# Layer 0 attention: the last two head pairs' scores on half-array tiles, two heads side by side

## The chip, the core and the metric

The kernel runs on one core of one Trainium2 chip. Times are device microseconds of one execution. A profile is one execution taken by the hardware profiler. Its engines are PE (the matmul array; PEld is its weight load), ACT (scalar engine), DVE (vector engine), POOL (GpSimd) and SP, which issues most of the transfers. All of them take their instructions in the order in which the program was built.

## What is computed

Two layers of a hybrid backbone over 2048 latent tokens with a prefix of 256 context tokens, width 1024. Layer 0 has two branches side by side: multi-head latent attention (eight heads) and bidirectional gated linear attention (four heads, chunks). Layer 1 is a neighbourhood attention. The change touches layer 0 alone:

```python
def block_attention(q, k, v, scale):        # 8 heads, q and k of width 64 + 32, v of width 64
    s = jnp.einsum('bqhd,bkhd->bhqk', qi, k) * scale
    p = jax.nn.softmax(s, axis=-1)
    return jnp.einsum('bhqk,bkhd->bqhd', p, v)
a_x = block_attention(q_x, concat([k_x, k_c]), concat([v_x, v_c]), scale)   # latents see all 2304 tokens
a_c = block_attention(q_c, k_c, v_c, scale)                                 # context sees itself
b_x, b_c = gla_bidirectional(...)                                           # the linear branch
a = a.reshape(bsz, n, A_WIDTH) * silu(za)
```

## The kernel before

`even_attention` (line 982) goes over four pairs of heads (j = 0 to 3). A pair has five query blocks: one of 256 context queries, which sees two key tiles of 128, and four of 512 latent queries, which see all 18. One key tile for both heads of a pair is called a step here: 74 steps a pair, 296 in all.

A step's scores (lines 1097 to 1099) are three matmuls for each head. Queries and keys are split into a high and a low half in a reduced-precision float format, and a score is high x high + high x low + low x high, each over the head's 96 columns as the rows of the array (97 in the first, whose extra row adds a per-query term to the exponent). The results go to one of three PSUM banks, tile `st`. ACT takes the exponential of each head's scores (`apt`, 14 buffers). DVE adds the exponentials of each head up over the key tiles (line 1088, tiles `acc0`, `acc1`).

The value products (line 1039, `tail`) run behind: when six steps are pending, four are flushed, eight matmuls in a row. Their operand is plain f32, which leaves two records in the trace for one matmul. They have 64 output columns, so the two heads lie in the two column halves of the array and of one bank (`av`, two buffers). When a block's last step has been flushed, `finish` (line 964) sums the denominators over partitions by two matmuls into a bank of its own (`den`, one buffer), takes the reciprocal as exp(-ln) with one Newton step, multiplies by the value product and by the gate on POOL, and stores to `RT`.

The linear attention (`gla`) is woven in. Its first phase (lines 797 to 877; eighteen chunks, tile `gl`, two banks) is written ahead of the attention but placed between its steps by the scheduler of the framework, which sets each engine's order when the program is built. Each chunk passes nine short groups of matmuls and, between them, ACT, DVE and small transfers; L861 is the one group in it that uses 64 rows of the array, and L870 the last of a chunk. A scan over chunks follows (lines 903 to 908, on POOL and DVE). The second phase reads the scan's results (`enter`, line 927, and `leave`, line 945) and is called, with the split of the output weights, by `hook` at each fourth step from step 174 on.

Of the kernel before, what the change touches and what calls it, by code (L numbers as in the profile page):

```python
# [17 lines left out]
P = 128  # L18
# [14 lines left out]
A_SCALE = A_QK ** -0.5  # L33

# [54 lines left out]
class Kern:  # L89
# [673 lines left out]
    def gla(self, gp, gs, g1, gd, pp, tag):  # L763
# [159 lines left out]
        def enter(c, qT, oi, zb):  # L923

            ps = bank()
            for h in range(H):
                nc.tensor.matmul(ps[:, h * P : h * P + P], qT[:, h, :], Dl[c][:, h, :], start=True, stop=True)
# [10 lines left out]
        def leave(c, oi, zb, ss):  # L938
# [3 lines left out]
            g.tensor_tensor(out=oi[:], in0=oi[:], in1=zb, op=ALU.mult)  # L942
            ps = bank()
            for h in range(H):
                nc.tensor.transpose(ps[:, h * P : h * P + P], oi[:, h * P : h * P + P], self.ident[:])
# [5 lines left out]
        def second():  # L951

            order = self.back_order()
            old, cur = None, fetch(order[0])
            for c in order[1:] + [None, None]:
                if old:
                    leave(*old)
                old = enter(*cur) if cur else None
                cur = fetch(c) if c is not None else None
                yield  # L960
# [21 lines left out]

    def even_attention(self, ap, pp, hook):
# [13 lines left out]
        def keys(j, p):  # L997

            K[j, p] = kh = ring[(3 * j + p) % 4]
            for a, b in parts(j, p):  # L1000
                nc.sync.dma_start(kh[:A_QK, :, a:b].bitcast(F32),
                                  self.KT[2 * j : 2 * j + 2, 0, :A_QK, p * W + a : p * W + b].rearrange("h p t -> p h t"))
                yield

        def low(j, p):
            L[j, p] = kl = self.tl(ap, [P, 2, W], "akl", F32R, bufs=3)
            for a, b in parts(j, p):
                nc.sync.dma_start(kl[:A_QK, :, a:b].bitcast(F32),
# [14 lines left out]
        def queries(j, q0, w):  # L1023

            q = self.tl(ap, [P, 4, w], "aq" if w == 512 else "aqc", F32R, bufs=2 if w == 512 else 1)
            nc.sync.dma_start(q[:A_QK, :, :].bitcast(F32), self.QT[2 * j : 2 * j + 2, :, :A_QK, q0 : q0 + w].rearrange("h z p t -> p (h z) t"))
# [4 lines left out]
        pend, late, O = [], [], {}  # L1031

        def tail(j, nb, n, kt, pts):

            w, kts = blocks[nb][1:]
            if n == 0:
                O[j, nb] = self.tl(pp, [P, 512], "av", bufs=2)
            for i in range(2):
                nc.tensor.matmul(O[j, nb][i * 64 : i * 64 + 64, :w], V[j, kt // TT][:, kt % TT, i * 64 : i * 64 + 64], pts[i][:, :w],  # L1039
                                 start=n == 0, stop=n == len(kts) - 1)  # L1040
            if n == len(kts) - 1:
                late.append([1, j, nb])

        def end(j, nb):
# [3 lines left out]
            self.finish(O.pop((j, nb))[:, :w], sums.pop((j, nb)), zt[:, :w], self.RT[j, :, q0 : q0 + w], w, ap, pp, ("den", 1))  # L1048

        def step_late():  # L1050
            for x in late:
                x[0] -= 1
                if x[0] <= 0:
                    end(*x[1:])
            late[:] = [x for x in late if x[0] > 0]

        early, sums, first = {}, {}, {}
        for j in range(4):
# [12 lines left out]
            for nb, (q0, w, kts) in enumerate(blocks):  # L1071
# [8 lines left out]
                acc = [self.tl(ap, [P, 512], f"acc{i}") if nb else self.tl(ap, [P, CTX], f"accc{i}", bufs=1) for i in range(2)]  # L1080

                def add(n, pts):
                    for i in range(2):
                        if n == 0:
                            first[i] = pts[i]
                        else:
                            a = first[i] if n == 1 else acc[i]
                            self.add = nc.vector.tensor_tensor(out=acc[i][:, :w], in0=a[:, :w], in1=pts[i][:, :w], op=ALU.add)  # L1088

                for n, kt in enumerate(kts):  # L1090
                    pts = []
                    kq = slice(kt % TT * P, kt % TT * P + P)
                    kh, kl = K[j, kt // TT], L[j, kt // TT]
                    for i in range(2):
                        qh, ql = Q[:, 2 * i, :], Q[:, 2 * i + 1, :]
                        ps = self.tl(pp, [P, 512], "st", bufs=3)
                        nc.tensor.matmul(ps[:, :w], kh[: A_QK + 1, i, kq], qh[: A_QK + 1, :w], start=True, stop=False)  # L1097
                        nc.tensor.matmul(ps[:, :w], kh[:A_QK, i, kq], ql[:A_QK, :w], start=False, stop=False)  # L1098
                        mm = nc.tensor.matmul(ps[:, :w], kl[:A_QK, i, kq], qh[:A_QK, :w], start=False, stop=True)  # L1099
                        pt = self.tl(ap, [P, 512], "apt", bufs=14)  # L1100
                        ex = self.act(pt[:, :w], ps[:, :w], AF.Exp, scale=A_SCALE)
                        pts.append(pt)
                    add(n, pts)
                    if n == len(kts) - 1:
                        sums[j, nb] = [a[:, :w] for a in acc]
                    pend.append((j, nb, n, kt, pts))
                    with self.tc.issue_after(mm.ins):
                        if len(pend) == 6:
                            step_late()
# [883 lines left out]
```

## Time and profile before

| | |
|---|---|
| time, median of three runs | 3546.57 us (3543.09 to 3547.34) |
| span of the profiled execution | 3541.8 us |
| PE busy in it | 3477.8 us, 98% |
| DVE, ACT, POOL busy | 2392.1, 1398.4, 1214.3 us |
| attention stage, first to last score matmul | 1058.5 to 1887.1 us |
| score matmuls in the trace (lines 1097 to 1099) | 576 of 512 columns on each line, 16 of 256 |
| records of value products | 1184 |

A group of the profile reads: line, engine, operation, tile written and tiles read, rows * columns of the array, shape of the operand, count, then busy time, mean length of one in ns, and idle time of the engine ahead of it with what ended it. In a row in order of time the first two numbers are the start and the length from the first start to the last end of what the row merges, in us.

### The profile page before, as it was taken

Reading aid. Unit: us, or ns where it says so; the run is one execution under the profiler, and the core shown is the slowest. Engines: PE = TensorE matmul, PEld = TensorE weight load, DVE = VectorE, ACT = ScalarE, POOL = GpSimd, SP = SyncE. Lnnn points to the kernel's source line nnn. Section 1 sums busy time; section 2 is a strip of 40 time slices with the busy share of each in tenths; the row PEclk is TensorE's granted clock in tenths of the full one; section 3 lists DMA queues with packets and bytes.
Section 4 is the critical chain, followed back from the end, with each engine's and each line's share of the span. In section 5 each row is a group of like instructions: output and inputs, shape, how many; then the busy total and the mean of one; then the engine's idle time right before and its main releaser. Section 6 shows DMA issues by size and latency. Waiting matters only on the chain. (4 is left out here: it accounts for less than half of the span.)

```text
span 3541.8 us, 53493 instructions
## 1 busy us (share of the span) xinstructions
PE 3477.8 (98%) x19260; PEld 2752.4 (78%) x19260; DVE 2392.1 (68%) x5020; ACT 1398.4 (39%) x2656; POOL 1214.3 (34%) x1363
## 2 busy tenths in 40 slices
PE   8999999999999999999999999999999999999999
PEld 6998999999996666656667888888898987555587
DVE  4677767888886777788765345455598883777821
ACT  5555451111116555555553134444422223555510
POOL 1433330111111222211321233333354544777743
PEclk9999999999999999999999999999999999999999
DMA  6555564222243343434543554555844348878664
GB/s 246 161 148 169 149 196 116 78 76 85 68 124 83 80 111 85 101 84 115 161 119 126 169 174 124 143 161 156 255 152 146 123 128 224 217 210 218 187 184 149
DMA packets 386914, 513.75 MB, mean 145 GB/s; under 512 B 61229, under 2 KB 264061, under 8 KB 380746
## 3 DMA queue, kind: packets, MB, share of 16 engines
q1 hardware_dynamic: 353242, 418.68, 41.3%
q0 software_dynamic: 21888, 62.56, 5.9%
q10 hardware_dynamic: 11520, 29.09, 2.3%
q8 instruction: 153, 2.51, 0.3%
q14 instruction: 111, 0.91, 0.1%
HBM read 330.61 MB, written 179.59 MB: 144 GB/s over the span
## 5 line engine op out<-in xcount | busy, mean ns | idle before, releaser
L1088 DVE TENSOR_TENSOR acc<-acc,apt 128x512 f32<-128x512 f32 x512 | 379.6, 772 | 142.2 <-ACT apt L106 139.5
L739 DVE TENSOR_REDUCE mm<-mx 128x1 f32<-128x512 f32 (+1 forms) x656 | 390.8, 628 | 87.8 <-PE mx L738 80.4
L106 ACT ACTIVATE apt<-st 128x512 f32<-128x512 f32 (+1 forms) x592 | 344.8, 594 | 247.3 <-PE st L1099 207.5
L1039 PE MATMUL av<-apt,av 128*64 128x512 f32 (+1 forms) x1184 | 270.0, 592 | 0.0
L1097 PE MATMUL st<-aq,akh 97*128 97x512 f32 x576 | 245.1, 426 | 1.0 <-ACT apt L106 1.0
L738 PE MATMUL mx<-mk,mq 96*128 96x512 f32 (+1 forms) x656 | 241.7, 371 | 0.0
L106 ACT ACTIVATE u<-gm 128x352 f32<-128x352 f32 (+1 forms) x144 | 70.8, 493 | 418.4 <-PE gm L131 182.6
L1098 PE MATMUL st<-aq,akh 96*128 96x512 f32 x576 | 228.2, 396 | 0.0
L1099 PE MATMUL st<-aq,akl 96*128 96x512 f32 x576 | 227.9, 396 | 0.0
L106 ACT ACTIVATE opt<-opt 128x930 f32<-128x930 f32 (+9 forms) x144 | 119.5, 831 | 254.5 <-POOL opt L1856 140.0
L1039 PEld LDWEIGHTS av<-apt,av 128*64 128x64 f32 x1184 | 80.1, 136 | 152.7 <-issue 149.7
L1554 DVE CUSTOM_DVE_ANT_1 mx<-mx,mtab 128x465 f32<-128x465 f32 (+12 forms) x576 | 180.3, 341 | 26.5 <-PE mx L1548 20.4
L1689 POOL TENSOR_TENSOR oacc<-oacc,opt 128x682 f32<-128x682 f32 (+9 forms) x144 | 170.3, 1200 | 40.6 <-ACT opt L106 39.1
L1818 DVE TENSOR_TENSOR opt<-st,tab 128x64 f32<-128x64 f32 (+10 forms) x576 | 142.3, 312 | 37.8 <-PE st L1654 33.2
L1097 PEld LDWEIGHTS st<-aq,akh 97*128 97x128 f32 x576 | 108.3, 188 | 72.6 <-issue 44.6
L1099 PEld LDWEIGHTS st<-aq,akl 96*128 96x128 f32 x576 | 109.5, 190 | 25.2
L738 PEld LDWEIGHTS mx<-mk,mq 96*128 96x128 f32 x656 | 123.3, 188 | 6.0
L1098 PEld LDWEIGHTS st<-aq,akh 96*128 96x128 f32 x576 | 109.9, 191 | 17.0
L106 ACT ACTIVATE x<-px,modB,modA 128x128 f32<-128x128 f32 x272 | 98.7, 465 | 55.9 <-PE px L362 32.5
L129 PE MATMUL gm<-w1h,hhi 128*128 128x512 f32 x288 | 115.1, 400 | 0.0
L1653 PE MATMUL st<-q,kt 128*128 128x480 f32 (+5 forms) x256 | 98.4, 386 | 16.8 <-DVE opt L1818 13.1
L131 PE MATMUL gm<-w0h,hlo 128*128 128x512 f32 x288 | 113.3, 393 | 1.5 <-DVE hlo L392 1.5
(602 smaller groups left out, 10275.6 us busy)
## 6 DMA issues: line engine op xcount, KB each, us to landing
q<-Q SPq DMA_DIRECT2D x48, 512.0 KB
H<-x ACTq DMA_DIRECT2D x36, 512.0 KB
adaw<-ada_w SPq DMA_DIRECT2D x64, 256.0 KB
x<-H SPq DMA_DIRECT2D x32, 512.0 KB
K1t<-okt POOLq DMA_DIRECT2D x32, 512.0 KB, 6.8
kt<-K1t SPq DMA_DIRECT2D x32, 512.0 KB
mtab<-rpb_q SPq DMA_DIRECT2D x16, 899.0 KB
QT<-qkhl SPq DMA_DIRECT2D x36, 384.0 KB
```

Of the source, the lines that this page charges most:

```text
L106: return self.nc.scalar.activation(out, in_, func, **kw)
L129: self.nc.tensor.matmul(out, lh(k), rh(k), start=j == 0, stop=False)
L738: mm = nc.tensor.matmul(ps[:, :w], q[:A_QK, (t % 6) * P : (t % 6) * P + P], k[:A_QK, k0 : k0 + w], start=True, stop=True)
L739: nc.vector.tensor_reduce(out=m[:, t, n : n + 1], in_=ps[:, :w], axis=AX.X, op=ALU.max)
L1039: nc.tensor.matmul(O[j, nb][i * 64 : i * 64 + 64, :w], V[j, kt // TT][:, kt % TT, i * 64 : i * 64 + 64], pts[i][:, :w], start=n == 0, stop ...
L1088: self.add = nc.vector.tensor_tensor(out=acc[i][:, :w], in0=a[:, :w], in1=pts[i][:, :w], op=ALU.add)
L1097: nc.tensor.matmul(ps[:, :w], kh[: A_QK + 1, i, kq], qh[: A_QK + 1, :w], start=True, stop=False)
L1098: nc.tensor.matmul(ps[:, :w], kh[:A_QK, i, kq], ql[:A_QK, :w], start=False, stop=False)
L1099: mm = nc.tensor.matmul(ps[:, :w], kl[:A_QK, i, kq], qh[:A_QK, :w], start=False, stop=True)
L1554: nc.vector.tensor_tensor_reduce(out=s, in0=s, in1=tb[:, ri : ri + rn, ci : ci + cn], scale=1.0, scalar=-3e38, op0=ALU.add, op1=ALU.max, a ...
L1689: self.psum = nc.gpsimd.tensor_tensor(out=a, in0=a, in1=pts[:, :, a0 - r0 : a1 - r0, :], op=ALU.add)
L1818: badd = nc.vector.tensor_tensor(out=pt[:, d[0], d[1]], in0=ps[:, d[0], d[1]], in1=tabs[j][i][:, ri : ri + rn, ci : ci + cn], op=ALU.add)
```

## The change

- For head pairs 2 and 3 (`HALVES`) a head's operands lie in 64 partitions, head 0 in the lower and head 1 in the upper half. A score is then five matmuls: three products of the 64 columns without rotary part (keys' low tile `kl` now holds high and low of these), one of 64 rows that holds two products of the 32 rotary columns, and one of 33 rows with the third and the extra row. The heads' matmuls alternate, each head into its own bank.
- The loads of these pairs are cut to match: six plus two transfers for a part of the keys instead of one plus one, twelve for a block of queries instead of two. POOL writes one row of ones into four key tiles.
- Score tiles get four banks. The bank comes from the denominators: ACT copies a block's value product out (`take`), the denominators are then summed into the same bank (`divide`), and `newton` does the rest.
- Exponentials of both heads share a tile, and so do the sums: one add of 1024 columns for a step.
- A flush is a chain in fixed order, scores wait in the program's order for the last flush and for the second phase's matmuls, and `hook` calls the second phase at a flush (`enter`, then `leave` of the chunk before) and at its middle (`scale`).

```diff
@@ even_attention: loads of pairs 2 and 3
+                if j >= HALVES:
+                    c = slice(p * W + a, p * W + b)
+                    for i in range(2):
+                        r, src = i * 64, self.KT[2 * j + i, :, A_NOPE:A_QK, c]
+                        for u, z in ((0, 0), (0, 1), (1, 0)):
+                            nc.sync.dma_start(kh[r + z * A_ROPE : r + z * A_ROPE + A_ROPE, u, a:b].bitcast(F32), src[z])
...
+                    for i in range(2):
+                        nc.sync.dma_start(kl[i * 64 : i * 64 + 64, :, a:b].bitcast(F32),
+                                          self.KT[2 * j + i, :, :A_NOPE, p * W + a : p * W + b].rearrange("z p t -> p z t"))
@@ scores
+                for k, kz, qz, n in ((kl, 0, 0, 64), (kl, 0, 1, 64), (kl, 1, 0, 64), (kh, 0, 2, 64), (kh, 1, 3, A_ROPE + 1)):
+                    for i in range(2):
+                        r = slice(i * 64, i * 64 + n)
+                        with self.tc.issue_after(mm.ins) if mm else ExitStack():
+                            mm = nc.tensor.matmul(ps[i], k[r, kz, kq], Q[r, qz, :w], start=qz == kz == 0 and k is kl, stop=k is kh and kz == 1)
@@ denominators
+    def take(self, o, pool, bufs):
+        y = self.tl(pool, [P, 512], "oy", bufs=bufs)[:, : o.shape[1]]
+        self.taken = self.act(y, o)
+        return y
+    def divide(self, o, acc, pool, bufs):
+        for h, a in enumerate(acc):
+            self.den = self.nc.tensor.matmul(o[h * 64 : h * 64 + 64], self.mtwos[:], a, start=True, stop=True)
...
+        def flush():
+            mm = None
+            jobs = [(ending, *x) for x in taken]
+            taken.clear()
+            for _ in range(4):
+                if pend and pend[0][2] == 0 and len(busy) == 2:
+                    break
+                if pend:
+                    jobs.append((tail, *pend.pop(0)))
...
+            for f, *a in jobs:
+                with self.tc.issue_after(mm.ins) if mm else ExitStack():
+                    mm = f(*a)
+            return mm
@@ the step
-                        ps = self.tl(pp, [P, 512], "st", bufs=3)
...
+                    ps = [self.tl(pp, [P, 512], "st", bufs=4)[:, :w] for _ in range(2)]
+                    mm = score(j, kt, Q, ps, w)
+                    pt = self.tl(ap, [P, 2, 512], "apt", bufs=7)
...
+                        self.add = nc.vector.tensor_tensor(out=acc[:, :, :w], in0=(first if n == 1 else acc)[:, :, :w], in1=pt[:, :, :w], op=ALU.add)
@@ hook
-                    if count[0] >= 174 and count[0] % 4 == 2:
+                    if count[0] >= 174 and (full or mid and said[0] == "A"):
                         with self.tc.issue_after(mm.ins), self.tc.issue_after(ex.ins), self.tc.issue_after(self.add.ins):
-                            next(slow, None)
+                            for _ in range(1 + (full and said[0] == "A")):
+                                said[0] = next(slow, None)
```

The order on PE shows what moves. First pair 3, before, between two flushes (`st` scores, `gl` the linear attention's second phase: `goi` is `leave`, `D` is `enter`):

```order
L1098 MATMUL st_16956<-aq_16634,akh_1774_10751 128x512
L1099 MATMUL st_16956<-aq_16634,akl_16423 128x512
L945 MATMUL gl_16905<-ident_58,goi_16703 128x128 x4
L927 MATMUL gl_16916<-D_1801_10808,gqT_16833 128x128 x4
L1097 MATMUL st_16962<-aq_16634,akh_1774_10751 128x512
```

and the same phase of the program now, at a flush (`av` value products):

```order
L1165 MATMUL st_16728<-aq_16582,akh_1773_10750 128x512
L1000 MATMUL av_16668<-accc_16511,mtwos_63 64x256 x2
L1098 MATMUL av_16750<-apt_16606,av_15555 64x512 x2
L1098 MATMUL av_16750<-apt_16623,av_15555 64x512 x2
L1098 MATMUL av_16750<-apt_16641,av_15555 64x512 x2
L1098 MATMUL av_16750<-apt_16657,av_15555 64x512 x2
L928 MATMUL gl_16767<-D_1802_10809,gqT_16698 128x128 x4
L949 MATMUL gl_16781<-ident_58,goi_16578 128x128 x4
L1165 MATMUL st_16798<-aq_16582,akl_16345 128x512
L1165 MATMUL st_16799<-aq_16582,akl_16345 128x512
```

The second phase has moved from between scores to between a flush and scores, and the scores of a step alternate between two banks (here 16798 and 16799).

In the first half of pair 2 the first phase of the linear attention cuts into flushes; this is one flush, now:

```order
L1098 MATMUL av_14949<-apt_15079,av_14761 64x512
L819 MATMUL gl_12093<-gG_12044,trr_10789 128x4x64
L820 MATMUL gl_12093<-ge_12046,trr_10789 128x4x64
L819 MATMUL gl_12093<-gG_12044,trr_10789 128x4x64
L820 MATMUL gl_12093<-ge_12046,trr_10789 128x4x64
L1098 MATMUL av_14949<-apt_15079,av_14761 64x512
L1098 MATMUL av_14949<-apt_15095,av_14761 64x512
L862 MATMUL gl_12108<-gqT_12066,gkT_12067 128x128
L1098 MATMUL av_14949<-apt_15095,av_14761 64x512
L1098 MATMUL av_14949<-apt_15119,av_14761 64x512 x2
L1098 MATMUL av_14949<-apt_15135,av_14761 64x512 x2
```

Its eight value products stand in pieces of one, two and five. Before, three flushes in the whole stage were cut after an odd number.

More of the change, by code (lines that the diff above doesn't have):

```diff
@@ L33 @@
 A_SCALE = A_QK ** -0.5
+HALVES = 2
 AXES = ((32, 8, 8), (64, 16, 16))
@@ L1047, in end @@
             nc.sync.dma_start(zt[:, :w], self.zaT[j, :, q0 : q0 + w])
[L1048 to L1057, printed above, removed]
+            rest.append((j, nb, o, y, rc, zt[:, :w]))
+            return self.den
@@ new lines, in behind @@
+        def behind(*last):
+            with ExitStack() as es:
+                for x in last:
+                    es.enter_context(self.tc.issue_after(x.ins))
+                for j, nb, o, y, rc, zt in rest:
+                    self.newton(o, y, rc)
+                    nc.gpsimd.tensor_tensor(out=rc, in0=rc, in1=zt, op=ALU.mult)
+                    q0, w, _ = blocks[nb]
+                    nc.sync.dma_start(self.RT[j, :, q0 : q0 + w], rc)
+                    busy.remove((j, nb))
+                rest.clear()
+                if late and not taken:
+                    taken.append((*late[0], self.take(late.pop(0)[2], ap, 1)))
```

146 lines of the change are left out of this document (93 added, 53 removed).

## The prediction

> **What bounds the kernel now.** The change lies in one stage, the layer 0 attention, so I read that stage first: busy time by head pair (columns: stretch, length, busy time and record count of PE, PEld, DVE, ACT, POOL, granted clock, DMA share, GB/s).
>
> ```profile
> 1058.50:1268.50 210.00, 207.77 (x1043) 130.90 (x1042) 155.48 (x219) 125.72 (x242) 42.44 (x49) 1.00 0.37 95
> 1268.50:1498.50 230.00, 227.46 (x1197) 144.59 (x1196) 169.37 (x236) 132.68 (x260) 62.78 (x65) 1.00 0.36 88
> 1498.50:1697.00 198.50, 197.43 (x931) 119.48 (x929) 167.10 (x286) 109.91 (x202) 35.94 (x33) 1.00 0.42 113
> 1697.00:1887.10 190.10, 190.10 (x902) 118.08 (x901) 131.16 (x280) 110.04 (x218) 42.91 (x42) 1.00 0.40 114
> ```
>
> PE is busy for 99% of the four pairs, at full clock (1.00). DVE, the next, has 69 to 84%, ACT 55 to 60%. The row of matmuls on PE sets the end of the stage, so the change is priced in PE time, and the other engines count where they make PE wait. The groups:
>
> ```profile
> L1039 PE MATMUL av<-apt,av 128*64 128x512 f32 (+1 forms) x1172 | 267.4, 592 | 0.0
> L1097 PE MATMUL st<-aq,akh 97*128 97x512 f32 x576 | 245.1, 426 | 1.0 <-ACT apt L106 1.0
> L861 PE MATMUL gl<-gqT,gkT 64*128 64x128 f32 x288 | 27.7, 289 | 0.0
> L870 PE MATMUL gl<-gu,gat 128*128 128x128 f32 x144 | 19.6, 279 | 1.9 <-DVE gat L866 1.8
> ```
>
> The mean there is a record's latency. What a matmul costs is the distance to the next start, in order of time:
>
> ```profile
> 1517.15 0.40 PE L1099 MATMUL st<-aq,akl 96*128 96x512 f32 x1
> 1517.48 1.16 PE L861 MATMUL gl<-gqT,gkT 64*128 64x128 f32 x14
> 1518.57 0.50 PE L1097 MATMUL st<-aq,akh 97*128 97x512 f32 x1
> 1518.90 0.40 PE L1098 MATMUL st<-aq,akh 96*128 96x512 f32 x1
> 1519.14 0.40 PE L1099 MATMUL st<-aq,akl 96*128 96x512 f32 x1
> 1519.37 0.40 PE L1097 MATMUL st<-aq,akh 97*128 97x512 f32 x1
> ...
> 1730.76 0.60 PE L945 MATMUL gl<-ident,goi 128*128 128x128 f32 x4
> 1731.20 1.06 PE L927 MATMUL gl<-D,gqT 128*128 128x128 f32 x8
> 1732.01 0.48 PE L1097 MATMUL st<-aq,akh 97*128 97x512 f32 x1
> ...
> 1735.37 0.40 PE L1099 MATMUL st<-aq,akl 96*128 96x512 f32 x1
> 1735.69 3.65 PE L1039 MATMUL av<-apt,av 128*64 128x512 f32 x16
> 1739.28 0.50 PE L1097 MATMUL st<-aq,akh 97*128 97x512 f32 x1
> 1739.62 0.39 PE L1098 MATMUL st<-aq,akh 96*128 96x512 f32 x1
> ```
>
> Three things are to be seen. A 512-column score matmul costs 0.235 us (0.24 and 0.23 between starts). The value product's 16 records, two for each of eight matmuls, take 3.59 us to the next start, 0.43 for two records: the heads, in column halves of the array, run side by side. And each change of tile form costs: 0.32 instead of 0.235 from score to value product, 0.34 for the first score after it.
>
> **The change part by part.**
>
> *Scores.* In pairs 2 and 3 a step (one key tile, two heads) goes from six matmuls one after another to five pairs on row halves. Whether such pairs overlap the trace shows at L861, the one form on 64 rows: 14 records, alternating between the halves, take 1.16 us, while eight records of L927 on the whole array take 1.06, or (1.06 - 0.28) / 7 = 0.11 each. Fourteen in a row would be 0.28 + 13 x 0.11 = 1.71; eight slots with a slow first of 0.1 are 1.15. So they overlap, in f32 at 128 columns; for these operands at 512 columns no row shows it. The bounds are a pair at 0.235 and at 0.47; I take 0.235, the end to which the nearest row belongs. There are 144 steps of 512 columns and four of 256, half as dear: 144 x 0.235 + 4 x 0.12 = 34.3 us saved.
>
> *Tile changes.* Scores in pairs 2 and 3 now have another form than the full-array matmuls of linear attention between them. Those were free: 1730.76 to 1732.01 is 1.25 us for 12 records of 0.11. Counted in the program's order from the first score to the last value product, changes of form go from 222 to 288: into value products and denominators 83 to 93, into scores 94 to 109, into other full-array work 13 to 60, into L861's 32 to 26. Prices from the rows: into a value product 0.14 (0.085 ahead of it and 0.05 on its first record), into scores 0.20 (0.10 of the 3.59, and 0.34 instead of 0.235 on the first), into L861 0.19, into full-array work 0.15, between those. 10 x 0.14 + 15 x 0.20 + 47 x 0.15 - 6 x 0.19 = +10.3 us.
>
> *Split flushes.* More flushes are now cut by other work after an odd number of matmuls, and the one without a partner has the array alone:
>
> ```profile
> 1403.90 3.60 PE L1039 MATMUL av<-apt,av 128*64 128x512 f32 x14
> 1407.43 0.66 PE L847 MATMUL gl<-ident,gqt 128*128 128x128 f32 x4
> 1408.02 1.07 PE L1039 MATMUL av<-apt,av 128*64 128x512 f32 x2
> 1409.02 0.66 PE L847 MATMUL gl<-ident,gkt 128*128 128x128 f32 x4
> ```
>
> Seven matmuls take 3.53 and the eighth 1.00, 4.53 against 3.59 for eight together; less the extra change of form that is 0.43 for each odd piece. Before there are 6 such pieces, now 25, and two of half the width: 19 x 0.43 + 0.4 = 8.6, and 0.7 for six odd pieces of paired scores: +9.3 us.
>
> *Four banks.* Heads now use banks two by two, so a step waits for both exponentials of the step two back. ACT's and PE's rows in order of time:
>
> ```profile
> 1614.05 1.55 ACT L106 ACTIVATE apt<-st 128x512 f32<-128x512 f32 x3
> ...
> 1614.30 0.40 PE L1099 MATMUL st<-aq,akl 96*128 96x512 f32 x1
> 1614.68 0.50 PE L1097 MATMUL st<-aq,akh 97*128 97x512 f32 x1
> 1615.01 0.40 PE L1098 MATMUL st<-aq,akh 96*128 96x512 f32 x1
> ...
> 1732.57 0.40 PE L1099 MATMUL st<-aq,akl 96*128 96x512 f32 x1
> ...
> 1733.00 3.40 ACT L106 ACTIVATE apt<-st 128x512 f32<-128x512 f32 x5 [0.41 <-PE st L1099]
> ```
>
> Three exponentials take 1.55, so they follow each other by 0.475 and one lasts 0.60; the first starts 0.03 after its matmul's end (1732.97 to 1733.00). A pair of banks started at t has its last matmuls at t + 0.94, done at 1.34, exponentials from 1.37 and 1.85, the second done at 2.45. A score that had waited for one began 0.05 after its end (1614.05 + 0.60 to 1614.68, with rounding) and its next came 0.33 later, 0.10 slow. The bank is free at 2.50; PE comes for it at 2 x 1.175 = 2.35. The third step of a run is held by 0.15 and up to 0.10 more, and all of PE's row behind it; the fourth is not. 28 flush cycles lie behind the linear attention's first phase: 28 x 0.20 = +5.6 us, bounds 0 and 37 x 0.25 = 9. ACT's throughput suffices: 0.95 us of exponentials in a step of 1.175.
>
> *Denominators.* They move from a bank of their own into the block's, after a copy on ACT. Inside the stage the copy is a flush old when PE comes; the 20 copies of 0.6 us fit into ACT's 40% of idle time. At the very end nothing covers it:
>
> ```profile
> 1889.50 3.65 PE L1039 MATMUL av<-apt,av 128*64 128x512 f32 x16
> 1892.99 1.03 PE L970 MATMUL den<-acc,mtwos 128*64 128x512 f32 x4
> ```
>
> From the last value record's start: 0.59 latency, 0.03, 0.60 copy, 0.05 = 1.28 instead of 0.43: +0.9 us.
>
> *Linear attention.* Its first phase ends later in the program: six of its 18 chunks now pass L870's matmuls in pair 2, three before.
>
> ```profile
> L870 PE MATMUL gl<-gu,gat x144: 272/275/377, 1136.5 to 1547.9; 128*128 128x128 f32 x144
> ```
>
> That is 24.2 us a chunk over 17 intervals. In the new pair 2 they lie 7.1 steps apart: 7.1 x (1.175 + 0.86) + 5 of its own matmuls + some 3.5 of changes and odd pieces = 23. PE comes up to 1.2 us early for each, if the chain over ACT, DVE and DMA can't go faster: bounds 0 and 8 us, I take +2, since the 1.9 us of L870 over all chunks show a chain that mostly keeps up.
>
> *Sums, loads.* One 1024-wide add takes the place of two:
>
> ```profile
> L1088 DVE TENSOR_TENSOR acc<-acc,apt x512: 674/691/2455, 1066.0 to 1888.1; 128x512 f32<-128x512 f32 x171
> ...
> L1258 DVE TENSOR_TENSOR aq<-pr,aq x2: 1224/1224/1225, 1844.6 to 1889.1; 128x1024 fp32r<-128x1024 f32 x2
> ...
> L1026 SPq DMA_DIRECT2D aq<-QT x3: 320/444/456, 1693.9 to 1798.4; - x3
> ```
>
> 1.22 against 2 x 0.69, on an engine with idle time: nothing on the path. SP issues 116 more transfers, at 0.44 some 50 us of its queue, spread over the last two pairs; queries are loaded a block (about 45 us) ahead, so 12 issues instead of 2 cost nothing. If that lead were gone, 10 x 0.44 = 4.4 us a block would show. POOL gets four one-row memsets, and is idle for 70% and more.
>
> *Sum.* -34.3 + 10.3 + 9.3 + 5.6 + 0.9 + 2 = -6.2 us. The profiled execution spans 3541.8 us, so 3535.6; the median of the runs lies 4.8 above that span: **3540.4 us**.
>
> **The rivals.** A measurement here tells a change from none at about 0.2%, 7.1 us, so below 3539.5 is faster and above 3553.7 slower.
>
> (1) *More of the saving stays* (18%). The third step isn't held, because exponentials end earlier than their records, and the chain keeps up: -34.3 + 10.3 + 9.3 + 0.9 = -13.8, 3533; if strict order also removes half of some 8 us in which PE stands now (the stage's 828.6 us against 821 of slots, changes and odd pieces added up as above), 3529. For it: ACT's slack. Against: the bank's arithmetic is only 0.15 short but short each time.
>
> (2) *Row halves don't overlap fully* (10%). [...] One by one, ten matmuls cost 2.35 against 1.41: 144 x 0.94 + 2 = +137 in place of -34.3, with no hold by banks: 3546.6 + 137 + 10 + 9 + 1 = 3704. The point from which the scores lose is a pair at 6 x 0.235 / 5 = 0.28. Of the 10%, four are for a partial loss, a pair at 0.31: 144 x (1.55 - 1.41) + 0.4 = +20.6, no hold, 3589 with the other terms. For it: no row for this form. Against: L861, whose slots are no longer than those of the whole array. [...]
>
> (3) *The wait moves to linear attention* (17%). In pair 2 PE stands ahead of chunk matmuls, since scores between them now pass in less time. From 13 us of such waits beside the forecast's it is slower: two us at each of six chunks and a few at the ends. Six at 3 us more: 3558. For it: 23 against 24.2. Against: chunks' pace before was set by PE's own order.
>
> **How the numbers follow.** Forecast 55%, own range 3532 to 3550, split about evenly by the bound, which lies 0.9 us below it. Faster: 0.25 of that, and 0.17 from (1): 0.42. Slower: 0.10, 0.11 and 0.03 from (2), (3) and the forecast: 0.24. The rest, 0.34, is the same. The range reaches from (1)'s far end with a margin for the unknown banks, 3523, to (3) with 8 us more, 3566; it leaves out (2) and some tails.
>
> **What would show it.** Right: pairs of score records some 0.01 us apart and pairs 0.235 apart; the four pairs at about 200, 221, 217 and 185 us, since chunks move from the first two to the third; a hold of 0.15 to 0.25 at each third step; odd pieces at 1.0 us for two records. Wrong: pairs at 0.3 or more; idle time of PE named after DVE or ACT at L871 and the transposes; a wait for a query's load.

## The result and the profile after

The changed kernel takes 3590.81 us (median of four runs, 3588.79 to 3594.35); the kernel before, run on the same chip, 3544.83. The ratio, here and below always to the kernel before on the same chip, is 1.0135, 95% interval 1.012 to 1.0149: **slower by 46 us**, where 6 us less were forecast, and outside the range of 3523 to 3566. The profiled execution spans 3587.0 us.

The busy time by head pair (stretch, length, then busy time and records of PE, PEld, DVE, ACT and POOL, granted clock, DMA share, GB/s), changed kernel:

```profile
1060.00:1258.80 198.80, 197.78 (x959) 123.33 (x958) 127.00 (x134) 118.03 (x225) 40.74 (x40) 1.00 0.35 89
1258.80:1479.00 220.20, 217.57 (x1099) 136.34 (x1097) 142.79 (x151) 124.81 (x243) 59.01 (x54) 1.00 0.34 85
1479.00:1733.10 254.10, 227.61 (x1402) 132.53 (x1401) 186.87 (x246) 122.65 (x247) 68.80 (x56) 0.94 0.39 104
1733.10:1932.20 199.10, 187.90 (x1204) 108.89 (x1203) 138.51 (x215) 105.21 (x226) 50.78 (x43) 0.97 0.42 120
```

About 200, 221, 217 and 185 us were forecast. The first two pairs came out as forecast; the third is 37 us longer, the fourth 14. In these two PE stands: it is busy for 90% and 94% instead of 99% and 100%, and the granted clock is below 1.00. What it stands for, in the list of PE's waits from 1300 us to the stage's end (who <- for whom, us in total, times, longest):

```profile
PE st L1165 <- ACT apt L107: 15.7, 4, 6.2
PE av L1000 <- ACT oy L107: 8.3, 3, 6.0
PE gl L949 <- POOL goi L943: 7.6, 1, 7.6
PE gl L804 <- DVE ge L865: 6.3, 2, 4.6
```

ACT is idle for half of these stretches, so "ACT" is not the cause. Its rows in order of time, each of which starts just before a long wait of PE ends (in brackets: idle time before, and what ended it):

```profile
1641.93 0.63 ACT L107 ACTIVATE gG<-wraw 128x512 fp32r<-128x512 f32 x1 [9.12 <-DMA wraw<-w_out]
...
1757.22 0.38 ACT L107 ACTIVATE oy<-av 128x256 f32<-128x256 f32 x1 [3.89 <-DVE rc L1012]
...
1884.91 0.63 ACT L107 ACTIVATE woh<-wraw 128x512 fp32r<-128x512 f32 x1 [9.05 <-DMA wraw<-w_out]
```

ACT kept to the order of its queue: PE had ended four scores by 1636.9, and their exponentials, behind the split at 1641.93, started at 1642.46. Twice it stands in the split of an output weight whose load could start only when DVE had finished the split before (there is one buffer `wraw`), once in the copy `take`, for whose single buffer `oy` DVE's Newton step is late. The first of the two is late because of DVE, which began its part of the previous split 5.6 us after ACT had done its own. At the second, near the stage's end, DVE was in time: SP issued the load 2 us later, behind three other loads, and ACT could start 7.3 us after that. The exponentials behind the splits, and the denominators behind the copy, are what PE then waits for. The longest wait, 7.6 us, is for the second phase's `scale`, which comes through DVE and POOL while DVE is still in the backward scan. Two more are long. One of 4.6 us, at 1500.5, is a chunk's own chain: DVE, which makes the `ge` that L804 waits for, had stood 3.9 us for the transfer `gE<-gqt`. One of 3.6 us, at 1685.7, stands behind ACT's copy in `leave`, whose tile `gsb` has its two buffers in common with the backward scan.

Why these meet now, two rows of single lines show (durations, then first and last start):

```profile
L871 PE MATMUL gl<-gu,gat x144: 272/275/377, 1138.6 to 1631.4; 128*128 128x128 f32 x144
...
L909 DVE TENSOR_TENSOR D<-gsb,fac x17: 687/689/1637, 1159.5 to 1687.6; 64x512 f32<-64x512 f32 x17
```

The first phase of linear attention ends at 1631 us; before it was 1548. Its last chunk stands at step 192 in the program's order, before at step 163.5, while splits and second phase still begin at step 174. So the last chunks, the scan (to 1688), the splits and the second phase's first chunks (from 1660) lie on top of each other. Who has no room for that is DVE. The scan's stretch by busy time, in the kernel before and then in the changed one:

```profile
1548.00:1614.00 66.00, 66.00 (x284) 38.56 (x283) 63.73 (x95) 35.76 (x60) 1.65 (x1) 1.00 0.22 58
```

```profile
1631.00:1690.00 59.00, 41.66 (x237) 24.75 (x238) 55.02 (x81) 19.18 (x38) 7.81 (x6) 0.84 0.25 71
```

DVE (third busy time) was full here before, 97%, and PE just did not wait. Now it is at 93%, with other work in the stretch and faster steps of PE beside it, and PE is busy for 71%.

Each long wait costs a second time. The one of 6.2 us, PE in order of time and then the granted clock by stretch:

```profile
1635.57 0.85 PE L1165 MATMUL st<-aq,akl 64*128 64x512 f32 x6
1636.25 0.62 PE L1165 MATMUL st<-aq,akh 64*128 64x512 f32 x4
1643.10 2.13 PE L1165 MATMUL st<-aq,akl 64*128 64x512 f32 x6 [6.22 <-ACT apt L107]
1644.60 1.48 PE L1165 MATMUL st<-aq,akh 64*128 64x512 f32 x4
```

```profile
1636.90:1640.50 3.60, 0.00 (x0) 0.00 (x0) 3.44 (x6) 0.00 (x0) 0.00 (x0) 0.99 0.10 12
1640.50:1647.30 6.80, 4.21 (x19) 3.22 (x20) 5.98 (x9) 3.82 (x8) 0.00 (x0) 0.50 0.33 109
1647.30:1654.00 6.70, 6.70 (x43) 3.20 (x40) 6.58 (x8) 3.20 (x7) 1.78 (x1) 1.00 0.13 39
```

Before the wait three pairs of scores take 0.68 us, behind it 1.50: the clock is granted at one half for 6.8 us, from 3.6 us after PE fell idle. There are six such stretches in the stage, 44 us in all, and none in the kernel before.

**The balance of pairs 2 and 3.** They are 51 us longer than forecast (453 against 402). Gaps of PE of more than 0.8 us beyond a record's normal distance make 39 us (before: none in these pairs). The 107 records at half clock took 28 to 30 us where the same forms at full clock take 17, 11 to 13 more, by how a record's normal distance is taken. That leaves 1 us or less: the other terms of the sum were right together, which does not say that each of them was.

### The profile page after: what moved, and what is told of

The parts are those of the page before. It is cut to its first block, busy times and chain, and to the rows that moved or that the text cites. A ratio compares the mean times of both kernels' runs of the same rounds, so it can differ in the third digit from the quotient of the medians.

```text
span 3587.0 us, 54227 instructions
## 1 busy us (share of the span) xinstructions
PE 3484.8 (97%) x19852; PEld 2738.3 (76%) x19852; DVE 2362.2 (66%) x4744; ACT 1392.5 (39%) x2676; POOL 1252.4 (35%) x1367
## 4 chain that ended last, share of the span: by engine, by line
PE 82%; DVE 6%; DMA 6%; issue 2%; ACT 2%; POOL 1%; SPq 0%; POOLq 0%; DVEq 0%; ACTq 0%
PE gm L132 8%; PE gm L130 8%; PE gm L131 8%; PE av L1098 7%; PE st L1165 4%; PE mx L739 4%; PE gm L191 2%; PE gm L192 2%; PE gm L193 2%; PE st L1751 2%; PE st L1156 2%; PE st L1158 2%; PE o L1781 2%; PE st L1157 2%; PE st L130 2%
## 5 line engine op out<-in xcount | busy, mean ns | idle before, releaser
L1201 DVE TENSOR_TENSOR acc<-acc,apt 128x1024 f32<-128x1024 f32 x256 | 354.3, 1384 | 164.6 <-ACT apt L107 157.6
L107 ACT ACTIVATE apt<-st 128x512 f32<-128x512 f32 (+1 forms) x592 | 327.5, 597 | 176.2 <-PE st L1158 91.0
L1098 PE MATMUL av<-apt,av 128*64 128x512 f32 (+1 forms) x1184 | 285.2, 602 | 0.0
L1165 PE MATMUL st<-aq,akl 64*128 64x512 f32 x864 | 153.3, 424 | 15.7 <-ACT apt L107 15.7
L1165 PEld LDWEIGHTS st<-aq,akl 64*128 64x128 f32 x864 | 88.8, 193 | 59.5 <-ACT apt L107 27.1
L1156 PE MATMUL st<-aq,akh 97*128 97x512 f32 x288 | 121.6, 422 | 1.0 <-ACT apt L107 1.0
L1157 PE MATMUL st<-aq,akh 96*128 96x512 f32 x288 | 114.6, 398 | 0.0
L1158 PE MATMUL st<-aq,akl 96*128 96x512 f32 x288 | 114.6, 398 | 0.0
L223 POOL TENSOR_TENSOR oss<-oss,mhalf 128x8 f32<-128x8 f32 x68 | 112.5, 1654 | 5.5
L130 PE MATMUL gm<-w0h,hhi 128*128 128x512 f32 x288 | 114.3, 397 | 0.0
```

Of the source, the lines that this page charges most:

```text
L107: return self.nc.scalar.activation(out, in_, func, **kw)
L130: self.nc.tensor.matmul(out, lh(k), rh(k), start=j == 0, stop=False)
L1098: mm = nc.tensor.matmul(O[j, nb][i * 64 : i * 64 + 64, :w], V[j, kt // TT][:, kt % TT, i * 64 : i * 64 + 64], pt[:, i, :w], start=n == 0, ...
L1156: nc.tensor.matmul(ps[i], kh[: A_QK + 1, i, kq], qh[: A_QK + 1, :w], start=True, stop=False)
L1157: nc.tensor.matmul(ps[i], kh[:A_QK, i, kq], ql[:A_QK, :w], start=False, stop=False)
L1158: mm = nc.tensor.matmul(ps[i], kl[:A_QK, i, kq], qh[:A_QK, :w], start=False, stop=True)
```

## The experiments

All kernels compute the whole function. Theory A: linear attention's late first phase, and the waits that come of it, eat the saving. Theory B: the 64-row tiles, or what they need, make the waits.

**Without 64-row tiles; then with their number of loads.**

```diff
-HALVES = 2
+HALVES = 4
```

> The restructured program with full-array scores in all four pairs (no 64-row tiles, and the loads of before). Theory A, the loss comes from linear attention: its first phase now ends 28 steps later in the program, so its last chunks, the scan, the weight splits and the second phase, which starts at a fixed step, meet in pairs 2 and 3, and PE waits for them. Here the first phase ends at step 200, later still, so the waits stay and the 34 us of the scores are given back: 3595 to 3625 us, with at least four PE waits above 3 us. Theory B, the 64-row tiles and what they need (twelve transfers for a block of queries, banks two by two) make the waits: 3535 to 3560, no wait above 3 us.

The second run adds to this, for keys and likewise for their low halves and the queries:

```diff
+                if j >= 2:
+                    for i in range(2):
+                        for m in range(3):
+                            s = slice(32 * m, 32 * m + 32)
+                            nc.sync.dma_start(kh[s, i, a:b].bitcast(F32), self.KT[2 * j + i, 0, s, p * W + a : p * W + b])
```

> As the run without 64-row tiles, but the loads of pairs 2 and 3 are cut into as many transfers as the 64-row tiles need (six and two for a part of the keys, twelve for a block of queries, by groups of rows and the same bytes). Theory A: the same time as the run without them, within 8 us. Theory B: SP's queue holds back what linear attention loads and stores; at least 15 us longer than that run.

3587.6 us without the tiles (ratio 1.0128, 1.0113 to 1.0143), 3587.4 with their loads. So the loss is there without a single 64-row tile, and SP's extra transfers cost nothing: Theory B falls. Theory A's time was too high too, by 7 us at its lower end, and three waits of 3 us or more are there where it named at least four; they stand at other places than in the changed kernel. PE's waits of the first run:

```profile
PE gl L928 <- ACT gsb L107: 17.4, 1, 17.4
PE av L1000 <- ACT oy L107: 7.1, 3, 5.3
PE gl L949 <- POOL goi L943: 3.0, 1, 3.0
```

With the first phase at step 200 the second phase runs into the scan even harder: one wait of 17.4 us, in which ACT's copy gets a `gsb` buffer only when the scan gives it back.

```profile
1701.78 2.18 ACT L107 ACTIVATE gsb<-gl,gn 128x128 f32<-128x128 f32 x8 [18.22 <-DVE gsb L908]
```

**What made the first phase late.** Which part of the change moved it was read from the order of programs built with one part undone at a time; these were not run, and no trace shows their steps. Scores tied to the last flush or not, a flush in fixed order or not: the last chunk stays at 192. Two adds instead of the joined one: 186. Three score banks instead of four: 159. In the traces of pairs 0 and 1 a chunk takes mostly 10 to 12 steps in the changed kernel, 8 in the kernel before. The likely reason, which no run shows by itself, is that the fourth bank lets the scheduler place scores further ahead, so that the chunks' short groups fall back. In pairs 0 and 1 nothing needs the fourth bank. So:

```diff
-                    ps = [self.tl(pp, [P, 512], "st", bufs=4)[:, :w] for _ in range(2)]
+                    ps = []
+                    for _ in range(2):
+                        tag = ("st", "st", "st2")[nst[0] % 3] if j < BANKS else ("st", "st2", "st", "st3")[nst[0] % 4]
+                        ps.append(self.tl(pp, [P, 512], tag, bufs=2 if tag == "st" else 1)[:, :w])
+                        nst[0] += 1
```

> The changed kernel with one edit: pairs 0 and 1 use three of the four score banks in rotation, pairs 2 and 3 all four. Built so, the scheduler places the first phase of linear attention as before: its last chunk ends at step 162 (before 163.5, changed kernel 192), changes of tile form in the stage fall from 290 to 245 and odd pieces of value products from 26 to 6. Theory A: the waits above 3 us go, the saving of the scores stays, 3515 to 3535 us, pairs of about 208, 228, 185 and 180 us. Theory B: pairs 2 and 3 keep their waits, 3575 to 3595.

3558.5 us (1.0048, 1.0032 to 1.0065): by the ratios 31 of the 46 us come back with this edit alone, and the trace has the last chunk at step 162. Not all of this is waits. From the first to the last score the profiled stage is 28 us shorter than in the changed kernel. PE's gaps above 0.8 us account for 17 of them (21 instead of 38), and about 10 are PE's own row, with the gaps and half of the busy time at half clock taken off. That row has 244 changes of tile form instead of 289 (222 in the kernel before) and 6 odd pieces of value products instead of 25 (6 before); at the prediction's prices the difference is 45 x 0.15 + 19 x 0.43 = 15 us. So the late first phase cost in two ways, and Theory A names one of them. The same edit in the program without 64-row tiles (`BANKS = HALVES = 4`):

> The restructured program with full-array scores in all pairs and three of the four score banks in rotation in all of them; the first phase ends at step 163 as before. Against the run without 64-row tiles it undoes the fourth bank alone. Theory A (the fourth bank made the first phase late): the waits above 3 us around the scan go, 3545 to 3562 us, and against the run with 64-row tiles and three banks in pairs 0 and 1 it shows what these tiles bring: 0 to 20 us. Rival (the 64-row tiles are what is left of the loss): 3535 to 3545, faster than that run by 13 us or more.

3568.1 us (1.0073, 1.0059 to 1.0087), 19.5 less than without the edit. So the fourth bank in pairs 0 and 1 is shown as the largest cause with the tiles; without them it makes 19.5 of 45 us, and the rest is not told apart. The first time lies between the two theories' ranges, the second above both: more waits than thought were left. Between these two runs the tiles bring about 9 us by the ratios. Pairs 2 and 3 of the run with tiles:

```profile
1501.40:1703.00 201.60, 193.68 (x1235) 112.55 (x1234) 165.03 (x215) 102.09 (x206) 41.76 (x37) 0.97 0.40 109
1703.00:1903.20 200.20, 188.79 (x1206) 109.76 (x1203) 138.53 (x215) 105.34 (x226) 50.85 (x43) 0.97 0.41 119
```

Still 8 and 11 us of idle PE, and 0.97 of the clock.

**The collisions undone, with the first phase left late** (splits from step 186 on and the last one a block later, the copy two steps later, the factors' exponential a chunk later, one scan operation on POOL):

```diff
-                    if count[0] >= 174 and (full or mid and said[0] == "A"):
+                    if count[0] >= 186 and (full or mid and said[0] != "B"):
...
-                if late and not taken:
+                if late and not taken and wait[0] < 0:
...
-                    eng.tensor_tensor(out=d[sl], in0=S[sl], in1=f[sl, 1, :]
+                    nc.gpsimd.tensor_tensor(out=d[sl], in0=S[sl], in1=f[sl, 1, :]
```

> The changed kernel, its first phase as late, with the collisions undone one by one: the weight splits start 12 steps later, two to a flush; the last of them comes one block later; the exponential of the decay factors is taken one chunk after their load; the copy of a value product waits two steps after a Newton step; POOL takes one of the three operations of the backward scan. Theory A: the waits at these five places (4.7, 6.4, 11.4, 6.1, 5.3 us in the changed kernel) fall below 2 us each, 3545 to 3562 us. Theory B: at most 10 us of the time comes back, 3578 to 3592.

3581.4 us (1.0113, 1.0098 to 1.0128), a miss for Theory A: 9 us came back. That is Theory B's range, though B's own reason had fallen with the runs before. The waits did not go, they changed their names:

```profile
PE st L1176 <- ACT apt L107: 10.0, 3, 6.4
PE gl L956 <- DVE goi L936: 7.2, 1, 7.2
PE gl L956 <- POOL goi L950: 6.1, 1, 6.1
PE av L1105 <- DVE rc L1019: 5.8, 2, 5.1
```

Behind most of this stands DVE, late with its adds, splits and the scan; and POOL's share of the scan made DVE wait up to 1.2 us for POOL in a chunk. Removing a wait at the one who waits was of little use while DVE was late.

**The waits left in the run with three banks, one by one.** The copy's buffer:

```diff
-                    taken.append((*late[0], self.take(late.pop(0)[2], ap, 1)))
+                    taken.append((*late[0], self.take(late.pop(0)[2], ap, 2)))
...
-            zt = self.tl(ap, [P, 512], "azt", bufs=2)
+            zt = self.tl(ap, [P, 512], "azt", bufs=1)
```

> As the run with three banks in pairs 0 and 1, and the copy of the value product has two buffers instead of one (the gate's tile one instead of two). Theory A: the wait of 6.1 us at the third change of pair, where ACT stands for the one buffer until DVE's Newton step has read it, falls below 2 us; 3548 to 3555 us. Rival: the Newton step's own end, which frees the value product's bank, is what is late; the wait moves to the next value product, 3556 to 3561.

3555.2 us (1.0039, 1.0025 to 1.0052), between the two forecasts. ACT's wait is gone, and the rival's mechanism was right: the wait is now PE's own, for the bank that the same Newton step frees.

```profile
PE av L1099 <- DVE rc L1013: 4.7, 1, 4.7
```

The splits' pace:

```diff
-                    for _ in range(6):
+                    for _ in range(3):
                         next(ws)
                         yield "W"
+                        yield "W"
                     for n, k in enumerate(second):
-                        if n % 4 == 3 and n < 36:
+                        if n % 3 == 2 and n < 36:
...
+                        with self.tc.issue_after(self.add.ins):
+                            for _ in last_w[0]:
+                                pass
```

> As the run with three banks in pairs 0 and 1, and the weight splits are paced by half at first (every second flush, then one in every three calls of the second phase) and the last one comes behind the last block. Theory A: the waits of 2.7 and 5.5 us, where ACT stands in a weight split for a load that could only start when DVE had done the split before, go; 3546 to 3553 us. Rival: ACT is late at these places for other reasons, 3556 to 3561.

3553.7 us (1.0035, 1.0021 to 1.0048), between the two forecasts. The wait of 2.7 us went; the last split's stayed, 5.2 us after 5.4. The likely reason is that it was tied to an add, which orders DVE's queue and not ACT's; tied to the last exponential, below, it went. Both remedies together, the Newton step ahead of the next add, and one scan operation on POOL:

```diff
+                      with self.tc.issue_after(self.newt.ins) if self.newt else ExitStack():
                         self.add = nc.vector.tensor_tensor(out=acc[:, :, :w], in0=(first if n == 1 else acc)[:, :, :w], in1=pt[:, :, :w], op=ALU.add)
```

> The changed kernel with three banks in pairs 0 and 1, two buffers for the copy, paced weight splits, the Newton step ahead of the next add on DVE, and one of the three operations of the backward scan on POOL. Theory A: no wait of PE above 3 us is left between the first score and the last, the clock stays granted in full, and the saving of the prediction appears: 3523 to 3540 us. Rival: something else than these waits holds the time, and 3545 or more is left.

3548.4 us (1.0019, 1.001 to 1.0028): better, but the rival's side. POOL's share made DVE wait for POOL about 1 us in each chunk of the scan. Mended:

```diff
+        with self.tc.issue_after(self.gat.ins):
+            scan(self.back_order(), slice(64, 128), nc.vector, "gsb")
...
+                        with self.tc.issue_after(self.ex.ins):
+                            for _ in last_w[0]:
+                                pass
```

> The run with all remedies, mended where its trace showed new waits: the backward scan is DVE's again but starts behind the last chunk's masks, and the last weight split is queued on ACT behind the last exponential. Theory A (waits of PE, and nothing else, ate the saving): the waits of 2.5 and 3.7 us at the scan and at the last split go, one of about 2.4 at the third change of pair stays; 3528 to 3541 us. Rival: something else holds the time, 3545 or more.

3543.6 us (1.0004, 0.9995 to 1.0013): level with the kernel before, between the two forecasts. The same with `HALVES = BANKS = 4`:

> The same remedies with full-array scores in all pairs and three of four banks throughout: the one difference to the run before is the 64-row tiles of pairs 2 and 3. By the prediction's prices, with 35 more changes of tile form, six odd pieces and the hold of the banks, the tiles bring 34 - 6 - 3 - 6 = 19 us: theory A 3545 to 3560 us, 12 to 22 above that run. Rival (the tiles bring nothing, since DVE and ACT can't follow the faster steps): within 6 us of it.

3550.0 us (1.0028, 1.0017 to 1.004): the tiles bring 6.4 us here by the medians and 8.5 by the ratios, whose intervals leave some 3 to 14. So they bring something, and the numbers don't decide between the rival's 6 and Theory A's 12. Added up over records in pairs 2 and 3, score matmuls take 20 us less with tiles than without, all other matmuls 5 more, and the waits above 0.8 us 5 more: PE, faster through its steps, waits more. So the rival's reason holds for a part, and the scores' price too.

**Two adds instead of the joined one**, in the run with three banks:

```diff
+                        for i in range(2):
+                            self.add = nc.vector.tensor_tensor(out=acc[:, i, :w], in0=(first if n == 1 else acc)[:, i, :w], in1=pt[:, i, :w], op=ALU.add)
```

> As the run with three banks in pairs 0 and 1, but two adds of 512 columns instead of one of 1024. The place of the first phase stays (its end at step 162). If the joined adds, which DVE cannot interrupt for a split or a mask, make the waits that are left: 3544 to 3552 us. If not: 3555 to 3563.

3566.2 us (1.0073, 1.0059 to 1.0086), slower: the joined add is not the trouble.

**The scan.** In the level kernel ACT's rows name what is late:

```profile
1599.62 1.09 ACT L108 ACTIVATE apt<-st 128x512 f32<-128x512 f32 x2 [5.96 <-DVE acc L1208]
...
1604.26 1.08 ACT L108 ACTIVATE apt<-st 128x512 f32<-128x512 f32 x2 [3.03 <-DVE acc L1208]
```

The exponential has no free buffer, since DVE is behind with its adds by as many steps as there are buffers, seven. So one chunk of the scan was dealt out behind every second add:

```diff
+                    if count[0] >= 163 and count[0] % 2:
+                        with self.tc.issue_after(self.add.ins):
+                            next(self.backward, None)
```

> As the run with mended remedies, but the backward scan is dealt out, one chunk behind every second step's add from step 163 to 197, instead of as fast as DVE gets to it. Theory A (the two waits of 2.3 and 2.6 us, where an exponential's buffer isn't free since DVE is behind with its adds, come from scan work packed between adds): both fall below 1.5 us and the clock stays granted there; 3533 to 3540 us. Rival: DVE has no room for the scan at this pace wherever it stands; the waits move within the scan's stretch, 3541 to 3548.

and with it, in a run of its own:

```diff
-                    eng.tensor_tensor(out=d[sl], in0=S[sl], in1=f[sl, 1, :]
+                    nc.gpsimd.tensor_tensor(out=d[sl], in0=S[sl], in1=f[sl, 1, :]
```

> As the run with the scan dealt out, and POOL takes the third of its three operations. Theory A: DVE has 0.69 us less to do for each chunk and POOL a step of time for it; 3531 to 3538 us. Rival: DVE waits for POOL to give the scan's buffer back, as before, and nothing is gained: at or above the run with the scan dealt out.

3539.7 us (0.9995, 0.9986 to 1.0003), and with POOL's share 3540.9 (0.9998, 0.9989 to 1.0006): both the same as the kernel before within their intervals. Both waits are gone, and a new one is there, at the first transposes of the second phase, whose operand comes through DVE and POOL. In the run without POOL's share:

```profile
PE gl L952 <- POOL goi L946: 10.1, 4, 6.1
PE av L1101 <- DVE rc L1015: 2.5, 1, 2.5
```

So splits and second phase begin one flush later, at step 178:

```diff
-                    if count[0] >= 174 and (full or mid and said[0] == "A"):
+                    if count[0] >= 178 and (full or mid and said[0] == "A"):
```

> As the run with the scan dealt out on DVE alone, but splits and second phase begin at step 178 instead of 174. Theory A (the wait of 6.3 us that appeared at the first transposes of the second phase is DVE still behind with its adds when the scan ends, and four steps more let it catch up): that wait falls below 3 us, 3531 to 3538 us, faster than before by 0.1 to 0.3%. Rival: DVE does not catch up in four steps, or the end of the second phase now stands in the way: 3539 or more.

**3534.8 us** (ratio 0.998, 0.9971 to 0.9989): in Theory A's range, and faster than both kernels. Its four pairs:

```profile
1061.10:1271.00 209.90, 208.09 (x1041) 130.91 (x1040) 138.65 (x145) 126.25 (x246) 54.80 (x49) 1.00 0.37 94
1271.00:1498.40 227.40, 224.65 (x1182) 143.54 (x1181) 151.23 (x165) 133.25 (x262) 70.40 (x63) 0.99 0.36 92
1498.40:1689.00 190.60, 187.01 (x1222) 107.86 (x1222) 162.63 (x208) 99.86 (x201) 40.36 (x32) 1.00 0.39 106
1689.00:1881.50 192.50, 187.20 (x1216) 109.28 (x1215) 144.24 (x230) 107.12 (x231) 58.23 (x47) 0.99 0.46 134
```

and what PE still waits for:

```profile
PE gl L952 <- POOL goi L946: 4.4, 4, 1.5
PE av L1101 <- DVE rc L1015: 2.9, 2, 2.6
PE gl L872 <- DVE gat L868: 1.8, 2, 1.5
```

The same restructure and tiles as in the changed kernel, and a difference of 55 us by the ratios, all of it order and buffers. That it now gains the 6 us of the forecast is chance. From the first to the last score PE's row is 18 us shorter than in the kernel before, with gaps above 0.8 us and half of the busy time at half clock taken off; the gaps (9 us instead of 2.5) and the half clock (about 3) take back 10.

## Why the prediction was wrong

**Scores: right.** The changed kernel's scores in order of time:

```profile
1786.48 0.97 PE L1165 MATMUL st<-aq,akl 64*128 64x512 f32 x6
1787.28 0.62 PE L1165 MATMUL st<-aq,akh 64*128 64x512 f32 x4
1787.74 0.86 PE L1165 MATMUL st<-aq,akl 64*128 64x512 f32 x6
1788.44 0.63 PE L1165 MATMUL st<-aq,akh 64*128 64x512 f32 x4
1788.90 1.13 PE L1165 MATMUL st<-aq,akl 64*128 64x512 f32 x6
1789.65 0.85 PE L1165 MATMUL st<-aq,akh 64*128 64x512 f32 x4
1790.11 1.09 PE L1165 MATMUL st<-aq,akl 64*128 64x512 f32 x6
1790.82 0.84 PE L1165 MATMUL st<-aq,akh 64*128 64x512 f32 x4
1791.59 0.65 PE L1098 MATMUL av<-apt,av 128*64 128x512 f32 x2
```

The second step lasts 1.16 us from start to start (1787.74 to 1788.90), five pairs of 0.23. In the first two steps the heads' records start 3 or 4 ns apart. Rival (2) is refuted, at 512 columns and for this operand. No run shows the pair at 0.31 that it priced as a partial loss: the pairs of these two steps took 0.23.

**Tile changes, split flushes, four banks on PE: right in sum, the hold of the banks too small.** The third step's second head starts 0.17 late, and from there the two heads run on displaced by one matmul, so that the last matmul of the fourth step runs alone. The four steps take 5.11 us up to the value product (1786.48 to 1791.59). From 1.26 for the first step, 3 x 1.16 for the others and 0.085 for the change to the value product, 4.83 would be due. So a flush is held by 0.28 where 0.20 was priced, and where ACT's copy of a block comes between the exponentials by some 0.3 more. Over 28 flushes and eight blocks that is an estimated 10 us instead of 5.6, beyond the bound of 9. With the waits and the half clock taken off, the balance of pairs 2 and 3 closes to about 1 us, so other terms must have cost some 5 us less than priced; which, no run tells.

**Denominators: right at the end, wrong inside.** The last denominator waits 0.89 us, forecast 0.9. But "inside the stage the copy is a flush old when PE comes" fails where the context block with its two steps follows a full block: two copies follow each other into one buffer, and DVE's Newton step between them is late. PE's waits for copies are 8.3 us, the end's included.

**Linear attention: the step that failed.** The forecast was +2 with bounds 0 and 8. Measured: 39 us of waits and 11 to 13 us at half clock in pairs 2 and 3, and undoing the shift alone brought 31 us back. The prediction had the fact in its hands, that more chunks end in pair 2 (seven by the trace, not six), and asked only whether a chunk's own chain can keep PE's pace. It did not ask what follows the last chunk: the scan, the splits and the second phase, whose start is a fixed step. It also took the shift for given, where its cause, the fourth bank, could be undone. Of the chunks' own waits, those at L871, which the "wrong" list named, are 0.4 us, those at L804 6.3.

**Rival (3), the wait moves to linear attention: right side, wrong place and size.** It put 13 us or more on the chunks' matmuls. Most of the waits are PE's scores and transposes, behind an ACT that stands for a weight or a copy, and behind DVE. The weight splits, which the change moved to each flush, had no term at all.

**Sums, loads: right for the loads** (3587.6 and 3587.4 with and without). The joined add takes 1.22 us at the median, as priced, and 1.38 on average; the adds before took 0.69 and 0.77, twice for a step. Splitting it again made the kernel slower, so nothing was lost there. "On an engine with idle time: nothing on the path" was too quick for DVE: a mean of 75% over the stage hid the 66 us of the scan at 97%, in the kernel before already. Faster steps of PE meet a DVE there that has nothing to give.

**Price of a wait: wrong throughout.** The prediction counted a wait of PE at its length. Behind nearly every wait of more than 2.5 us half the clock was lost for 3.4 to 10.2 us more.

## What to carry to other kernels

A buffer more is a change of the program's order wherever a scheduler decides it: compare where each stage of the interleaved work ends before and after, in steps of the main loop, and then follow what starts at a fixed step or needs a tile from there. An engine with 75% mean load can be full for 66 us; sum up its work stretch by stretch, and look for the late engine behind the one that a wait names, since a remedy at the waiting one only moves the wait. Where PE sets the time, price a wait at its length and the half clock behind it on top: here 3.4 us or more of half clock followed 40 of 40 waits from 2.7 us on, and 11 of 15 from 2.0 to 2.7.

## What the runs showed of the hardware

The clock was granted at one half behind most waits of PE from 2.0 us on. Over the 16 profiled kernels, gaps of PE between the stage's first and last score were followed by a stretch at half clock, beginning 1.4 to 5.1 us after PE fell idle, in 40 of 40 cases from 2.7 us on, 11 of 15 from 2.0 to 2.7, and 10 of 60 from 1.0 to 2.0; in seven of these ten another gap lay within 5 us. The stretches were 3.4, 6.8, 10.2 or 17.1 us long, multiples of 3.4. One of the short ones, in the run with all remedies before they were mended, PE in order of time and the stretches:

```profile
1591.48 0.63 PE L1166 MATMUL st<-aq,akh 64*128 64x512 f32 x4
1594.48 2.13 PE L1166 MATMUL st<-aq,akl 64*128 64x512 f32 x6 [2.38 <-ACT apt L108]
1595.99 1.48 PE L1166 MATMUL st<-aq,akh 64*128 64x512 f32 x4
```

```profile
1592.00:1594.30 2.30, 0.11 (x2) 0.00 (x0) 2.24 (x3) 0.47 (x1) 0.00 (x0) 1.00 0.00 0
1594.30:1601.10 6.80, 6.62 (x29) 5.01 (x30) 6.42 (x7) 3.88 (x8) 2.08 (x1) 0.50 0.01 2
```

A wait of 2.38 us, and 6.8 us at half clock behind it, in which PE was busy for 6.62: half of that, 3.3 us, is an estimate of what the clock cost, more than the wait.
